# A trunk layer on one core: gate-and-up weights split 256 columns at once, and two of the second sub-layer's weight sums made in DRAM

## The chip, the cores and the metric

The kernel runs on one core of one Trainium2 chip. A core has a matrix engine (PE, with its weight loads listed as PEld), a vector engine (DVE), an activation engine (ACT), GpSimd (POOL) and a sync engine (SP) that issues transfers; each works through its own queue of instructions in a fixed order, and they wait for each other by semaphores. Data lie in DRAM, in SBUF (128 partitions) and in PSUM, the eight banks into which PE sums. The metric is the device time in microseconds (us) of one execution.

## The reference

One layer over 512 tokens of width 1024, all in float32, with three sub-layers, each between two RMS norms:

```python
x = x + 1/2 * PostNorm(SwiGLU_1(PreNorm(x)))   # gate and up: 1024 -> 2 x 2816, down: 2816 -> 1024
x = x +       PostNorm(Mixer(PreNorm(x)))      # pooling heads and sliding-window attention
x = x + 1/2 * PostNorm(SwiGLU_2(PreNorm(x)))

def swiglu(h, w_gu, w_down):
    gate, up = split(h @ w_gu, 2)
    return (silu(gate) * up) @ w_down
```

The change concerns the product `h @ w_gu` of the two SwiGLU sub-layers, named f1 and f2 in the kernel.

## The kernel before

**Numbers in two parts.** PE multiplies in a short format. So each float32 operand is split into a high part (a rounding copy, line 125 on ACT or 127 on DVE) and a low part (operand minus high part, line 128, on DVE or POOL), and each product of two 128x128 by 128xN blocks takes three matmuls (`mm3`, lines 304 to 306): high times high, high weight times low token part, low weight times high token part. The third of three is the first that needs the low part of the weights.

**Gate and up.** The columns of both halves are taken in 11 chunks of 256 (`CH`). Chunk 0 is multiplied block by block while the tokens are being normed (`block`, line 446). For the other ten, gate and up, each cut into two halves of features, make a two by two block matrix: a and b of gate, c and d of up, 512 features x 256 columns each, 0.5 MB. The tokens make the other one. Seven products take the place of eight (a form of Strassen's scheme by Winograd). Their weight operands are a (product 1), b (2), d (4), and four sums: s1 = c + d (5), s2 = s1 - a (6), s4 = b - s2 (3) and s3 = a - c (7). The sums of tokens are made once (`token_sums`); the sums of weights are made for each chunk by DVE (`makers`, lines 177 to 198), in chunk 1 by POOL.

The loop of lines 488 to 513 takes 128 columns at a time: of the seven products, each of 12 matmuls of 128x256 that sum into half a PSUM bank, in the order 1, then product 4 of the columns before (`finish`), then 2, 5, 6, 3, 7. Between them ACT and DVE copy partial results out of PSUM and add them up; DVE's sum after product 7 is line 512.

**Order of the weights' work.** `Weights` holds a list of operands in the order of use and makes an operand's parts when it is `AHEAD` = 4 operands ahead of the product being written; the two pools of parts hold `WB` = 12 tiles of 128x512. Loads are issued by SP, `run_ahead` loads ahead, each of 512 features x 256 columns, into `BIG` = 8 tiles of 0.5 MB. `behind` (line 435) lets a piece of work be issued only after certain steps. PE's queue stands in the order of the program; the other engines' queues, outside `in_order()`, stand in the order that a scheduler found while the program was built.

**The start.** Four blocks of 128 tokens are loaded, normed and turned (`first_steps`). The norm's root r_a of each block is made on POOL (line 279), and DVE then scales the block (line 323). POOL also makes low parts of the first weights there. r_a3, the root of the last block, stands ahead of half of the first columns' products.

Of the kernel before, what the change touches and what calls it, by code (L numbers as in the profile page):

```python
# [19 lines left out]
P = 128  # L20
S = 512
# [18 lines left out]
WB = 12  # L40
AB = 8
HB = 25
BIG = 8
AHEAD = 4
# [4 lines left out]
def shape_consts():  # L49
    """What depends on the shapes alone: the band of the sliding window, the count of tokens at the  # L50
    start of a trailing window, and the frequencies of the rotation."""
    c = np.zeros((P, CW), np.float32)
    i, j = np.arange(P)[:, None], np.arange(2 * P)[None, :]
    diff = i + P - j
    c[:, :256] = np.where((diff >= 0) & (diff < P), 0.0, NEG)
    for g, w in enumerate(WINDOWS):
        n = np.minimum(np.arange(16) + 1, w)
        c[:, 256 + 16 * g : 272 + 16 * g] = (np.float32(w) / n.astype(np.float32))[None, :]
    e = -np.arange(0, ROT, 2, dtype=np.float32) / np.float32(ROT)
    c[:, -8:] = np.power(np.float32(500000.0), e)[None, :]  # L60
    return c
# [3 lines left out]
def trunk_layer(  # L65
# [11 lines left out]
    pp = ctx.enter_context(tc.tile_pool(name="pp", bufs=8, space=PSUM))  # L77
# [6 lines left out]
    def bank(name):  # L84
        return pp.tile([P, 512], F32, tag="ps", name=name)
# [7 lines left out]
    # ---- weights, in the order of their use: each is split into two parts of 12 significant bits  # L93
    class Weights:
        def __init__(self):
# [3 lines left out]
            self.hi, self.lo = nc.scalar, nc.vector  # L99

        def add_load(self, key, src, shape):
            self.loads.append((key, src if isinstance(src, list) else [(slice(0, P), src)], shape))

        def add(self, name, make):
            """An operand: make() gives it in float32 once the loads added so far are there."""
            self.index[name] = len(self.todo)
            self.todo.append((name, len(self.loads), make))
# [8 lines left out]

        def make_to(self, n):
            while self.made < min(n, len(self.todo)):
                name, need, make = self.todo[self.made]
                self.load_to(need + self.run_ahead)  # L120
                src = make()
                hi = wp.tile(list(src.shape), F32R, tag="hi", name=f"{name}_hi")
                lo = wp.tile(list(src.shape), F32R, tag="lo", name=f"{name}_lo")
# [21 lines left out]
    def add_plain(key, src, shape, picks):  # L145
        W.add_load(key, src, shape)
        for name, at in picks:
            W.add(name, lambda at=at: W.raw[key][at])

    def add_gate_up(name, w_gu, c):  # L150
        def load(m, kh):
            c0 = m * FF + c * CH
            src = w_gu[0, kh * 512 : (kh + 1) * 512, c0 : c0 + CH]
            W.add_load(f"{name}_{c}{m}{kh}", src.rearrange("(k p) c -> p k c", p=P), [P, 4, CH])

        cut = [(slice(None), slice(None), slice(j * P, (j + 1) * P)) for j in range(2)]
        if c == 0:
            for m in range(2):
                load(m, 0)
                load(m, 1)  # L160
                for i in range(4):
# [3 lines left out]
                        lambda m=m, kh=kh, j=j: W.raw[f"{name}_0{m}{kh}"][cut[j]],  # L165
                    )
            return
        for m in range(2):
            for kh in range(2):
                load(m, kh)  # L170
        box = {}

        def parts(j):
            return [W.raw[f"{name}_{c}{m}{kh}"][cut[j]] for m in range(2) for kh in range(2)]

        def a11(j):
            r = parts(j)
            if j == 0:
                box["s1"] = big(f"{name}_{c}s1", (P, 4, CH))
            eng = nc.gpsimd if c == 1 else nc.vector  # L180
            eng.tensor_tensor(box["s1"][cut[j]], r[2], r[3], ALU.add)
            eng.tensor_tensor(r[2], r[0], r[2], ALU.subtract)  # L182
            return r[0]

        def s2(j):
            r = parts(j)
            nc.vector.tensor_tensor(r[0], box["s1"][cut[j]], r[0], ALU.subtract)
            return r[0]

        def s4(j):  # L190
            r = parts(j)
            nc.vector.tensor_tensor(r[1], r[1], r[0], ALU.subtract)  # L192
            return r[1]

        makers = (
            (1, a11), (2, lambda j: parts(j)[1]), (5, lambda j: box["s1"][cut[j]]), (6, s2), (3, s4),
            (7, lambda j: parts(j)[2]), (4, lambda j: parts(j)[3]),
        )
        for j in range(2):
            for p, make in makers:  # L200
                W.add(f"{name}_{c}{j}p{p}", lambda make=make, j=j: make(j))

    def add_ffn(name, w_gu, w_down):
        for c in range(NCH):
            add_gate_up(name, w_gu, c)
        for k in range(KF):
            add_plain(
                f"{name}_d{k}", w_down[0, k * P : (k + 1) * P, :], [P, D],
                [(f"{name}_d{k}{n}", (slice(None), slice(n * 512, (n + 1) * 512))) for n in range(2)],
            )  # L210

    def add_in(name, c0, w, kk, per):
        for q in range(KD // kk):
            src = w_in[0, q * kk * P : (q + 1) * kk * P, c0 : c0 + w]
            picks = [
                (f"{name}{(q * kk + i) // per}", (slice(None), i if per == 1 else slice(i, i + per)))
                for i in range(0, kk, per)
            ]
            add_plain(f"{name}_{q}", src.rearrange("(k p) c -> p k c", p=P), [P, kk, w], picks)

    # ---- what stays on chip
# [20 lines left out]
    rows = cp.tile([12, P], F32, name="rows")  # L242
# [5 lines left out]

    add_ffn("f1", ffn1_w_gu, ffn1_w_down)
    add_in("wq", PW, 512, 2, 1)  # L250
    add_in("wkv", 2 * PW, 256, 4, 2)
    add_in("wu", 0, 512, 2, 1)
    for n in range(2):
        ns = slice(n * 512, (n + 1) * 512)
        for q in (2, 3, 0, 1):
# [6 lines left out]
            picks = [(f"wo{n}{2 * q + i}", (slice(None), i)) for i in range(2)]  # L262
            add_plain(f"wo{n}_{q}", src, [P, 2, 512], picks)
# [12 lines left out]
    def power(ms, name):  # L276
        """ms ** -0.5"""
# [9 lines left out]
    def squares(parts, mult, name, split=False):  # L287
        """Sums of (mult * part) ** 2 of two halves of a block of tokens."""
        ss2 = sm.tile([P, 2], F32, tag="ss2", name=f"ss2_{name}")
        for n in range(2):  # L290
            if n == 1 and split:
                junk = wk.tile([P, 512], F32, tag="sg", bufs=2, name=f"j_{name}{n}")
# [8 lines left out]
    def mm3(ps, wl, xr, first, last, open_=False):  # L301
        """ps += w.T @ x from the parts of both."""
# [10 lines left out]
    # ---- norm of a block of tokens, and its transpose  # L313
# [37 lines left out]
    def post_norm(t, parts, g, scale, name, dst=None):  # L351
        """x += scale * norm(parts) * g for a block of tokens."""
# [30 lines left out]
    def evacuate(src, t, kh, xq):  # L383
        at = slice((t % 2) * P, (t % 2 + 1) * P)
        hi, lo = xq[0][kh, t // 2]
        nc.scalar.copy(hi[:, :, at], src)
        nc.vector.tensor_tensor(lo[:, :, at], src, hi[:, :, at].bitcast(F32), ALU.subtract)

    def keep(src, t, kh, xq):
        at = slice((t % 2) * P, (t % 2 + 1) * P)  # L390
        for q in range(2):
            nc.scalar.copy(xq[1][kh, t // 2][q][:, :, at], src[:, 2 * q : 2 * q + 2, :])
# [7 lines left out]
    def token_sums(xq, name):  # L400
        """The sums of quarters that the seven products take."""
# [5 lines left out]
        for q in range(2):  # L407
            b11, b12, b21, b22 = (full[i][q] for i in ((0, 0), (0, 1), (1, 0), (1, 1)))
            nc.vector.tensor_tensor(b11, b12, b11, ALU.subtract)
            nc.vector.tensor_tensor(b12, b22, b12, ALU.subtract)  # L410
            nc.vector.tensor_tensor(b22, b22, b11, ALU.subtract)
            nc.vector.tensor_tensor(b21, b21, b22, ALU.subtract)
# [9 lines left out]
    def product_late(ps, w, xt, first, last):  # L422
        """As product(), with the low part of the tokens last."""
# [6 lines left out]
    def product(ps, w, xt, first=True, last=True):  # L430
        for k in range(4):
            mm3(ps, (w[0][:, k], w[1][:, k]), (xt[0][:, k], xt[1][:, k]), first and k == 0, last and k == 3, True)
# [8 lines left out]
    def gate_up(name, xq, hs, between):  # L441
        """silu(x @ gate) * (x @ up), transposed. The first columns block by block as the tokens
        come; then, for 128 columns of both, the two by two blocks (gate, up; tokens) from seven
        products (Winograd's form of Strassen's)."""
# [20 lines left out]
        W.more(4)  # L465
        for j in range(2):
            sg = wk.tile([P, S], F32, tag="sg", bufs=2, name=f"{name}_s0{j}")
            nc.scalar.activation(sg, banks[0, j], AF.Silu)
            h = slot(f"{name}_h0{j}")
            nc.vector.tensor_tensor(h, banks[1, j], sg, ALU.mult)  # L470
            hs.append(h)

# [7 lines left out]

        def finish():
            ps, w, h, sg = last
            product(ps[:, a], w, xs_[4], False)
            on_dve.append(nc.vector.tensor_tensor(h[:, a], ps[:, a], sg[:, a], ALU.mult).ins)
            nc.vector.tensor_tensor(h[:, b], h[:, b], sg[:, b], ALU.mult)
            hs.append(h)

        for c in range(1, NCH):
            if c == NCH - 1:
                W.run_ahead = 2  # L490
            for j in range(2):
                nm = f"{name}_{c}{j}p"
                px, py, pz = (bank(f"{name}_{i}{c}{j}") for i in "xyz")
                sg = wk.tile([P, S], F32, tag="sg", bufs=2, name=f"{name}_s{c}{j}")
                h = slot(f"{name}_h{c}{j}")
                product(px[:, a], operand(f"{nm}1"), xs_[1], last=False)
                on_act.append(nc.scalar.copy(sg[:, a], px[:, a]).ins)
                if last:
                    finish()
                    if c == NCH - 1 and j == 0:  # L500
# [666 lines left out]
```

## Time and profile before

| | |
|---|---|
| time, median of 3 runs | 871.38 us (869.79 to 871.93) |
| profiled execution, span | 871.8 us |
| PE busy | 848.6 us, 97% |
| DVE busy | 628.8 us, 72% |
| ACT busy | 428.1 us, 49% |
| POOL busy | 104.6 us, 12% |
| moved by DMA | 87.35 MB, 100 GB/s on the mean |
| f1: start and first columns | 0 to 40.27 us |
| f1: gate and up, ten chunks | 40.27 to 241.95 us |
| f1: down | 242.1 to 363.7 us |
| mixer and output | to 516.4 us |
| f2: first columns | 516.4 to 543.5 us |
| f2: gate and up, ten chunks | 543.5 to 745.1 us |
| f2: down | 745.1 to 867 us |

The stages are told apart by what PE multiplies. The span is that of the one execution that the hardware profiler took; the median is that of three other runs. A row of a timeline has start, duration (both us), engine, line, operation, what it writes and reads by the program's names with buffer numbers left out, partitions x elements; then, in brackets, how long the engine had been idle and which instruction released it.

### The profile page before, as it was taken

How to read it: one execution, taken by the hardware profiler on the slowest of the kernel's cores; microseconds unless marked ns; L12 is line 12 of the kernel's file. 1: busy time of each engine (PE TensorE's matmuls, PEld its weight loads, DVE VectorE, ACT ScalarE, POOL GpSimd, SP SyncE). 2: the span in 40 equal slices, each digit the busy share in tenths (PEclk: the TensorE clock that was granted, in tenths of full speed). 3: DMA queues.
4: the chain of work that ended last, by engine and by line, in shares of the span. 5: the costliest groups of instructions: out<-in, count | busy, mean ns of one | idle time of the engine just before them, and what ended most of it. 6: DMA issues, size and time to landing. Idle time of an engine off the chain costs nothing. (4 is left out here: it accounts for less than half of the span.)

```text
span 871.8 us, 14391 instructions
## 1 busy us (share of the span) xinstructions
PE 848.6 (97%) x5633; PEld 775.9 (89%) x5633; DVE 628.8 (72%) x1177; ACT 428.1 (49%) x923; POOL 104.6 (12%) x124
## 2 busy tenths in 40 slices
PE   7999999999999999999989989999999999999996
PEld 5999999999988888888767779999999999888885
DVE  6988888888893223855998879988888888942214
ACT  6555555555583222637653356555555555832211
POOL 4300000000000000136464334000000000000000
PEclk9999999999999999999999999999999999999999
DMA  9333333333363333202023401333333333642002
GB/s 306 89 97 98 97 98 97 111 118 127 105 232 122 97 97 95 73 26 51 24 64 108 143 24 50 97 98 97 98 97 97 108 119 114 227 135 73 1 1 97
DMA packets 62448, 87.35 MB, mean 100 GB/s; under 512 B 3492, under 2 KB 50220, under 8 KB 62380
## 3 DMA queue, kind: packets, MB, share of 16 engines
q1 hardware_dynamic: 62380, 86.44, 31.0%
q8 instruction: 44, 0.72, 0.3%
q14 instruction: 24, 0.20, 0.1%
HBM read 84.33 MB, written 2.10 MB: 99 GB/s over the span
## 5 line engine op out<-in xcount | busy, mean ns | idle before, releaser
L304 PE MATMUL f_acc<-f_d_hi,f_hp_hi 128*128 128x512 f32 x352 | 137.4, 390 | 0.0
L306 PE MATMUL f_acc<-f_d_hi,f_hp_lo 128*128 128x512 f32 x352 | 137.1, 389 | 0.0
L305 PE MATMUL f_acc<-f_d_lo,f_hp_hi 128*128 128x512 f32 x352 | 137.1, 389 | 0.0
L128 DVE TENSOR_TENSOR f_d_lo<-f_d_raw,f_d_hi 128x512 fp32r<-128x512 f32 x88 | 58.9, 690 | 100.4 <-ACT f_d_hi L125 100.4
L125 ACT CAST f_d_hi<-f_d_raw 128x512 fp32r<-128x512 f32 x88 | 53.2, 621 | 108.6 <-PE f_acc L306 107.2
L304 PEld LDWEIGHTS f_acc<-f_d_hi,f_hp_hi 128*128 128x128 f32 x352 | 66.1, 188 | 13.7
L306 PEld LDWEIGHTS f_acc<-f_d_hi,f_hp_lo 128*128 128x128 f32 x352 | 66.1, 188 | 13.6
L305 PEld LDWEIGHTS f_acc<-f_d_lo,f_hp_hi 128*128 128x128 f32 x352 | 66.1, 188 | 13.6
L510 ACT ACTIVATE f_s<-f_s 128x512 f32<-128x512 f32 x40 | 25.3, 632 | 49.3 <-DVE f_s L509 49.2
L505 ACT COPY f_h<-f_y 128x256 f32<-128x256 f32 x40 | 14.9, 373 | 58.0 <-PE f_y L306 58.0
L279 POOL TENSOR_TENSOR r_f2po<-ms_f2po,half 128x1 f32<-128x1 f32 x4 | 2.2, 550 | 328.1 <-DVE ms_f2po L284 328.1
L279 POOL TENSOR_TENSOR r_f1po<-ms_f1po,half 128x1 f32<-128x1 f32 x4 | 2.2, 548 | 321.8 <-DVE ms_f1po L284 321.8
L512 DVE TENSOR_TENSOR f_h<-f_x,f_h 128x256 f32<-128x256 f32 x40 | 17.0, 424 | 31.3 <-PE f_x L306 31.3
L530 DVE TENSOR_TENSOR f_hp_lo<-f_h,f_hp_hi 128x512 fp32r<-128x512 f32 x44 | 27.9, 687 | 0.0
L192 DVE TENSOR_TENSOR f_raw<-f_raw,f_raw 128x512 f32<-128x512 f32 x40 | 27.5, 687 | 0.0
L304 PE MATMUL po<-wo_hi,yT_hi 128*128 128x512 f32 x64 | 26.4, 412 | 0.0
L305 PE MATMUL po<-wo_lo,yT_hi 128*128 128x512 f32 x64 | 25.8, 403 | 0.0
L306 PE MATMUL po<-wo_hi,yT_lo 128*128 128x512 f32 x64 | 25.7, 401 | 0.0
L507 ACT COPY f_s<-f_x 128x256 f32<-128x256 f32 x40 | 14.9, 373 | 21.9 <-PE f_x L306 21.9
L182 DVE TENSOR_TENSOR f_raw<-f_raw,f_raw 128x512 f32<-128x512 f32 x36 | 24.7, 687 | 0.0
L529 ACT CAST f_hp_hi<-f_h 128x512 fp32r<-128x512 f32 x44 | 24.6, 617 | 0.0
L298 ACT ACTIVATE j_f2po<-f_acc 128x512 bf16<-128x512 f32 x8 | 4.8, 597 | 27.3 <-PE f_acc L306 27.3
(1541 smaller groups left out, 3044.5 us busy)
## 6 DMA issues: line engine op xcount, KB each, us to landing
f_raw<-in_ffn_w_gu SPq DMA_DIRECT2D x88, 512.0 KB, 5.4
f_d_raw<-in_ffn_w_down SPq DMA_DIRECT2D x44, 512.0 KB, 4.5
x<-in_x SPq DMA_DIRECT2D x4, 512.0 KB, 8.2
wq_raw<-in_w_in SPq DMA_DIRECT2D x4, 512.0 KB, 3.6
wu_raw<-in_w_in SPq DMA_DIRECT2D x4, 512.0 KB, 3.7
wo_raw<-in_w_out SPq DMA_DIRECT2D x8, 256.0 KB, 4.0
wo_raw<-in_w_out SPq DMA_DIRECT2D x4, 512.0 KB, 3.6
out<-x SPq DMA_DIRECT2D x8, 256.0 KB, 2.1
```

Source lines behind the costliest of these rows:

```text
L125: nc.scalar.copy(hi, src)
L128: self.lo.tensor_tensor(lo, src, hi.bitcast(F32), ALU.subtract)
L182: eng.tensor_tensor(r[2], r[0], r[2], ALU.subtract)
L192: nc.vector.tensor_tensor(r[1], r[1], r[0], ALU.subtract)
L304: nc.tensor.matmul(ps, wh, xh, start=first, stop=False, skip_group_check=open_)
L305: nc.tensor.matmul(ps, wh, xlo, start=False, stop=False, skip_group_check=open_)
L306: nc.tensor.matmul(ps, wlo, xh, start=False, stop=last, skip_group_check=open_)
L505: on_act.append(nc.scalar.copy(h[:, b], py[:, a]).ins)
L510: on_act.append(nc.scalar.activation(sg, sg, AF.Silu).ins)
L512: on_dve.append(nc.vector.tensor_tensor(h[:, b], px[:, a], h[:, b], ALU.add).ins)
L529: nc.scalar.copy(hi[:, j], hs[2 * q + j])
L530: nc.vector.tensor_tensor(lo[:, j], hs[2 * q + j], hi[:, j].bitcast(F32), ALU.subtract)
```

## The change

Four things change together; the matmuls keep their number and shape.

First, a chunk's products take all 256 columns: the parts of an operand are tiles of 128x1024 (`WB` 6 of them, `AHEAD` 2), one product is 24 matmuls into two neighbouring banks (`bank_pair`, `use_banks`), and each of ACT's and DVE's steps on partial results is done for both halves, in one instruction or in two. The order of products is now 1, product 4 of the chunk before, 5, 2, 6, 3, 7.

Second, the signs of the tokens are turned (`evacuate`, `keep`, `token_sums`, and a scale of -1 in the activations), so that the weight sums become s2 = s1 + a, s4 = s2 + b: sums only. Chunk 1 of f1 has its sums on DVE like the others.

Third, for f2 the sums s1 and s3 of chunks 1 to 10 are made in DRAM: for each of four steps, POOL issues a copy of half of one operand's columns from DRAM to DRAM (512x1280, 2.62 MB, line 285) and two adding DMAs of 256x1280 (line 288). f2 then loads five blocks of 0.5 MB a chunk (a, b, s1, s3, d) in place of four.

Fourth, the weights of the mixer, the output projection and the down projections are also split in tiles of 128x1024.

```diff
-WB = 12
+WB = 6
-HB = 25
+HB = 24
-AHEAD = 4
+AHEAD = 2
...
+        made = sums_of.get(name)
+        if made:
+            cols = slice((c - 1) * CH, c * CH)
+            for i in made:
+                src[i] = made[i][:, cols].rearrange("(k p) c -> p k c", p=P)
...
+        def s1():
+            if not made:
+                raw[key["s1"]] = big(f"{key['s1']}", shape)
+                plus("s1", "c", "d")
+                plus("c", "a", "c")
+            return raw[key["s1"]]
+
+        def s2():
+            return plus("s1", "s1", "a") if made else plus("a", "s1", "a")
+
+        def s4():
+            return plus("s1", "s1", "b") if made else plus("b", "a", "b")
+
+        s3 = "s3" if made else "c"
+        for p, make in (
+            (1, lambda: raw[key["a"]]), (5, s1), (2, lambda: raw[key["b"]]), (6, s2), (3, s4),
+            (7, lambda: raw[key[s3]]), (4, lambda: raw[key["d"]]),
+        ):
+            W.add(f"{name}_{c}p{p}", make)
...
+    def sum_in_dram(step):
+        i, m, kh = (("s1", 1, 1), ("s3", 0, 0))[step // 2]
+        half = (FF - CH) // 2
+        at = slice(step % 2 * half, (step % 2 + 1) * half)
+        to = sums_of["f2"][i][:, at]
+        c0 = CH + step % 2 * half
+        nc.gpsimd.dma_start(to, ffn2_w_gu[0, :512, FF + c0 : FF + c0 + half])
+        part = ffn2_w_gu[0, kh * 512 : (kh + 1) * 512, m * FF + c0 : m * FF + c0 + half]
+        for rows in (slice(0, 256), slice(256, 512)):
+            nc.gpsimd.dma_start(to[rows], part[rows], accum_op=ALU.add)
...
+    def product(pair, half, w, xt, first=True, last=True):
+
+        for j in range(2):
+            at = slice(j * P, (j + 1) * P)
+            for k in range(4):
+                mm3(
+                    pair[:, j, half], (w[0][:, k, at], w[1][:, k, at]), (xt[0][:, k], xt[1][:, k]),
+                    first and k == 0, last and k == 3, True,
+                )
...
         for c in range(1, NCH):
             if c == NCH - 1:
                 W.run_ahead = 2
+            nm = f"{name}_{c}p"
+            if name == "f1" and 2 <= c < 6:
+                sum_in_dram(c - 2)
+            px = bank_pair(f"{name}_x{c}")
...
+            product(px, a, operand(f"{nm}1"), xs_[1], last=False)
+            on_act.append(nc.scalar.copy(sg[:, :, a], px[:, :, a]).ins)
+            if last:
+                finish()
...
+            product(px, a, operand(f"{nm}7"), xs_[7], False, False)
+            for j in range(2):
+                on_dve.append(nc.vector.tensor_tensor(h[j][:, b], px[:, j, a], h[j][:, b], ALU.add).ins)
+            last = (px, operand(f"{nm}4"), h, sg)
```

How the queues of POOL and DVE stand is set when the program is built, at three places as follows. POOL at the start of the program, before (r_a0 to r_a3 are the roots of the four blocks of tokens, f1_c the first columns' weights):

```order
L279 TENSOR_TENSOR r_a0_155<-ms_a0_153,half_96 128x1
L279 TENSOR_TENSOR r_a1_167<-ms_a1_165,half_96 128x1
L128 TENSOR_TENSOR f1_c000_lo_197<-f1_000_raw_102,f1_c000_hi_196 128x512
L128 TENSOR_TENSOR f1_c001_lo_205<-f1_001_raw_104,f1_c001_hi_204 128x512
L128 TENSOR_TENSOR f1_c010_lo_211<-f1_000_raw_102,f1_c010_hi_210 128x512
L128 TENSOR_TENSOR f1_c011_lo_215<-f1_001_raw_104,f1_c011_hi_214 128x512
L279 TENSOR_TENSOR r_a2_239<-ms_a2_237,half_96 128x1
L279 TENSOR_TENSOR r_a3_260<-ms_a3_258,half_96 128x1
L128 TENSOR_TENSOR f1_c111_lo_263<-f1_011_raw_109,f1_c111_hi_262 128x512
```

and after (sum_s1 and sum_s3 are the sums in DRAM; line 285 is a step's copy, 288 its adds):

```order
L285 DMA sum_s1_104<-in_ffn2_w_gu 512x1280
L285 DMA sum_s1_104<-in_ffn2_w_gu 512x1280
L285 DMA sum_s3_105<-in_ffn2_w_gu 512x1280 x2
L318 TENSOR_TENSOR r_a0_159<-ms_a0_157,half_96 128x1
L318 TENSOR_TENSOR r_a1_171<-ms_a1_169,half_96 128x1
L288 DMA sum_s1_104<-in_ffn2_w_gu 256x1280 x2
L156 TENSOR_TENSOR f1_c00_lo_201<-f1_000_raw_106,f1_c00_hi_200 128x4x128
L288 DMA sum_s1_104<-in_ffn2_w_gu 256x1280 x2
L156 TENSOR_TENSOR f1_c01_lo_209<-f1_001_raw_108,f1_c01_hi_208 128x4x128
...
L318 TENSOR_TENSOR r_a2_237<-ms_a2_235,half_96 128x1
L288 DMA sum_s3_105<-in_ffn2_w_gu 256x1280 x2
L318 TENSOR_TENSOR r_a3_258<-ms_a3_256,half_96 128x1
```

The four copies stand ahead of r_a0, and each step's adds, which wait until that step's copy is complete, stand between the roots and the low parts of the first weights; the third step's stand ahead of r_a3.

DVE where chunk 2 of f1 gives way to chunk 3, before (20 and 21, 30 and 31 are the two halves of 128 columns of chunks 2 and 3; 3s1 is a sum of weights, 30p1_lo the low part of product 1's operand, h and s partial results, x, y and z banks of PSUM):

```order
L128 TENSOR_TENSOR f1_21p4_lo_1014<-f1_211_raw_761,f1_21p4_hi_1013 128x512
L181 TENSOR_TENSOR f1_3s1_1038<-f1_310_raw_767,f1_311_raw_1030 128x4x128
L128 TENSOR_TENSOR f1_30p1_lo_1042<-f1_300_raw_763,f1_30p1_hi_1041 128x512
L182 TENSOR_TENSOR f1_310_raw_767<-f1_300_raw_763,f1_310_raw_767 128x4x128
L128 TENSOR_TENSOR f1_30p2_lo_1059<-f1_301_raw_765,f1_30p2_hi_1058 128x512
L509 TENSOR_TENSOR f1_s21_962<-f1_y21_960,f1_s21_962 128x256
L512 TENSOR_TENSOR f1_h21_963<-f1_x21_959,f1_h21_963 128x256
L187 TENSOR_TENSOR f1_300_raw_763<-f1_3s1_1038,f1_300_raw_763 128x4x128
L485 TENSOR_TENSOR f1_h21_963<-f1_h21_963,f1_s21_962 128x256
```

and after (h20 and h21 are chunk 2's two halves):

```order
L568 TENSOR_TENSOR f1_s2_769<-f1_y2_829,f1_s2_769 128x2x256
L572 TENSOR_TENSOR f1_h20_770<-f1_x2_768,f1_h20_770 128x256
L572 TENSOR_TENSOR f1_h21_771<-f1_x2_768,f1_h21_771 128x256
L211 TENSOR_TENSOR f1_3s1_989<-f1_3c_raw_726,f1_3d_raw_951 128x1024
L156 TENSOR_TENSOR f1_3p1_lo_960<-f1_3a_raw_722,f1_3p1_hi_959 128x1024
L535 TENSOR_TENSOR f1_h20_770<-f1_h20_770,f1_s2_769 128x256
L535 TENSOR_TENSOR f1_h21_771<-f1_h21_771,f1_s2_769 128x256
L211 TENSOR_TENSOR f1_3c_raw_726<-f1_3a_raw_722,f1_3c_raw_726 128x1024
L156 TENSOR_TENSOR f1_3p5_lo_993<-f1_3s1_989,f1_3p5_hi_992 128x1024
```

The low part of chunk 3's first operand stood four rows ahead of the sum out of x21 (line 512), which follows product 7. It now stands behind the two such sums (line 572) and s1.

DVE at the end of f2's first columns, before (f2t are sums of tokens, c10 and c11 the banks of the first columns' up half, h00 and h01 their results):

```order
L412 TENSOR_TENSOR f2f101_5767<-f2f101_5767,f2f111_5769 128x512
L470 TENSOR_TENSOR f2_h00_6223<-f2_c10_5992,f2_s00_6221 128x512
L128 TENSOR_TENSOR f2_10p3_lo_6236<-f2_101_raw_6189,f2_10p3_hi_6235 128x512
L419 TENSOR_TENSOR f2t6_lo_6160<-f2f111_5769,f2t6_hi_6159 128x512
L419 TENSOR_TENSOR f2t4_lo_6164<-f2f100_5766,f2t4_hi_6163 128x512
L470 TENSOR_TENSOR f2_h01_6227<-f2_c11_6017,f2_s01_6225 128x512
```

and after:

```order
L461 TENSOR_TENSOR f2t6_lo_5600<-f2f111_5209,f2t6_hi_5599 128x512
L461 TENSOR_TENSOR f2t4_lo_5604<-f2f100_5206,f2t4_hi_5603 128x512
L156 TENSOR_TENSOR f2_1p2_lo_5668<-f2_1b_raw_5629,f2_1p2_hi_5667 128x1024
L461 TENSOR_TENSOR f2t4_lo_5604<-f2f101_5207,f2t4_hi_5603 128x512
L519 SCALAR_TENSOR_TENSOR f2_h00_5653<-f2_c10_5426,f2_s00_5651 128x512
L519 SCALAR_TENSOR_TENSOR f2_h01_5657<-f2_c11_5455,f2_s01_5655 128x512
```

The rows that read the banks c10 and c11 stand behind all low parts of the token sums and a split of 128x1024; before, some of the token sums came after them.

More of the change, by code (lines that the diff above doesn't have):

```diff
@@ L185, in s2 @@
[L185 to L201, printed above, removed]
+        src = {"a": block(0, 0), "b": block(0, 1), "c": block(1, 0), "d": block(1, 1)}
@@ L545, in down_proj @@
                     h_pair(k // 2 + 1)
-                w = [W.get(f"{name}_d{k}{n}") for n in range(2)]
+                w = in_halves(W.get(f"{name}_d{k}"))
             for t in range(NT):
```

238 lines of the change are left out of this document (126 added, 112 removed).

## The prediction

> **What bounds the kernel now.** The page comes first: busy time by engine, then the slices.
>
> ```profile
> PE 848.6 (97%) x5633; PEld 775.9 (89%) x5633; DVE 628.8 (72%) x1177; ACT 428.1 (49%) x923; POOL 104.6 (12%) x124
> ...
> PE   7999999999999999999989989999999999999996
> ...
> DMA  9333333333363333202023401333333333642002
> GB/s 306 89 97 98 97 98 97 111 118 127 105 232 122 97 97 95 73 26 51 24 64 108 143 24 50 97 98 97 98 97 97 108 119 114 227 135 73 1 1 97
> ```
>
> PE is busy for 848.6 of 871.8 us. A change can win by issuing fewer matmuls, which this one doesn't, or out of the other 23 us; it can lose wherever it makes PE wait. The DMA is full in one slice only, the first. The windows say where the 23 us lie; columns are the busy time of each engine with its instructions, then the granted clock, the DMA share and GB/s.
>
> ```profile
> 0.00:22.00 22.00, 17.48 (x97) 12.89 (x98) 14.92 (x28) 13.13 (x32) 10.17 (x16) 0.92 0.96 306
> 22.00:40.27 18.27, 17.32 (x145) 16.91 (x144) 18.00 (x24) 11.20 (x24) 7.74 (x6) 1.00 0.35 103
> 100.00:150.00 50.00, 50.00 (x419) 50.00 (x418) 42.12 (x80) 27.17 (x55) 0.00 (x0) 1.00 0.27 85
> 441.00:516.40 75.40, 67.08 (x290) 53.37 (x289) 64.22 (x98) 30.18 (x67) 33.31 (x34) 0.93 0.28 85
> 516.40:543.50 27.10, 25.60 (x210) 24.84 (x208) 24.98 (x37) 15.72 (x37) 12.83 (x10) 1.00 0.19 60
> 543.50:745.10 201.60, 201.60 (x1683) 201.60 (x1681) 172.21 (x323) 111.26 (x226) 0.00 (x0) 1.00 0.34 108
> ```
>
> In gate and up PE has no gap: 1683 matmuls in 201.60 us, 0.12 us each, so a chunk of 256 columns (168 matmuls) is 20 us and one of its products (24 matmuls, both 128-column halves) 2.87 us. PE idles at the start (4.5 and 1 us) and in mixer and output (8.3 and 1.5). DVE has slack but it is 0.85 busy in gate and up, so what matters is the order in which its queue stands.
>
> **The new forms.** All products keep their 24 matmuls per 256 columns; PE does as much as before. Four splits of 128x512 become two of 128x1024, on DVE and ACT. The rows for DVE's sizes, and the place where one product hands over to the next, before:
>
> ```profile
> 109.27 0.28 PE L306 MATMUL f_x<-f1t_hi,f_40p_lo 128*128 128x256 f32 x1
> 109.39 0.28 PE L304 MATMUL f_x<-f1b_hi,f_41p_hi 128*128 128x256 f32 x1
> 109.62 0.28 PE L306 MATMUL f_x<-f1b_hi,f_41p_lo 128*128 128x256 f32 x1
> ```
>
> ```profile
> 106.26 0.69 DVE L128 TENSOR_TENSOR f_41p_lo<-f_raw,f_41p_hi 128x512 fp32r<-128x512 f32 x1
> ...
> 109.58 0.42 DVE L512 TENSOR_TENSOR f_h<-f_x,f_h 128x256 f32<-128x256 f32 x1 [0.93 <-PE f_x L306]
> 109.93 0.68 DVE L187 TENSOR_TENSOR f_raw<-f_4s,f_raw 128x512 f32<-128x512 f32 x1
> 110.52 0.42 DVE L485 TENSOR_TENSOR f_h<-f_h,f_s 128x256 f32<-128x256 f32 x1
> ```
>
> The last matmul of product 7 starts at 109.27, product 1 of the next columns at 109.39; its third matmul, the first with a low part, at 109.62, 0.23 later. DVE's sum out of PSUM (L512) starts 0.19 after the next product begins and gives way after 0.35 (109.58 to 109.93) though it lasts 0.42; a 128x512 gives way after 0.59 and lasts 0.68. By these slopes 128x1024 gives way after some 1.1 us and lasts 1.2 (estimates from these rows). Before, the low part of product 1 (the row at 106.26) began 3.4 us ahead of need.
>
> **Each chunk's first product: +26 in the first sub-layer, +17 in the second.** As built, the queue of DVE puts the low part of the next chunk's product 1 behind the two sums (now L572) that wait for the end of product 7, the product just before it; in the first sub-layer also behind the sum s1 (L211). Time is counted from the start of product 1: the sums start at 0.2 and 0.55, s1 at 0.9, the low part at 2.0, done at 3.2. Needed at 0.23. PE waits 3.0 us. Without s1 the low part starts at 0.9, done at 2.1: 1.85. What follows isn't late again, since DVE works on while product 1 and the held-back product 4 run, 5.7 us. In the first sub-layer chunk 2 has no s1 there (1.85) and chunks 3 to 10 do (8 x 3.0): 25.9. In the second s1 comes loaded: 9 x 1.85 = 16.7. Nothing hides these, for PE has no other product that it could take first. From below, the wait would be nothing only if DVE's order weren't fixed; it is. From above, 3.4 and 2.2, if a wait costs DVE another 0.35. The two sums that come ready from DRAM relieve a DVE that was hidden anyway: nothing.
>
> **The start: +26.** POOL before (its timeline), with the row of its longest wait:
>
> ```profile
> 11.07 6.28 POOL L128 TENSOR_TENSOR f_c_lo<-f_raw,f_c_hi 128x512 fp32r<-128x512 f32 x4 [0.84 <-ACT f_c_hi L125]
> 18.50 0.66 POOL L279 TENSOR_TENSOR r_a<-ms_a,half 128x1 f32<-128x1 f32 x1 [1.16 <-DVE ms_a L284]
> 20.96 1.27 POOL L279 TENSOR_TENSOR r_a<-ms_a,half 128x1 f32<-128x1 f32 x1 [1.80 <-DVE ms_a L284]
> 22.20 1.28 POOL L128 TENSOR_TENSOR f_c_lo<-f_raw,f_c_hi 128x512 fp32r<-128x512 f32 x1
> ```
>
> ```profile
> 22.27 3.46 DVE L323 SCALAR_TENSOR_TENSOR xn_a<-x,r_a,g 128x512 f32<-128x512 f32 x2 [0.45 <-POOL r_a L279]
> 30.31 0.68 DVE L387 TENSOR_TENSOR f1b_lo<-tr_f,f1b_hi 128x512 fp32r<-128x512 f32 x1
> ```
>
> ```profile
> 40.27 0.28 PE L304 MATMUL f_x<-f1b_hi,f_10p_hi 128*128 128x256 f32 x1
> ```
>
> The fourth block of tokens hangs on r_a3 on POOL (20.96 to 22.23), DVE scales it at 22.27, and gate and up start at 40.27, 18 us behind. The source puts the DMAs that make the sums into chunks 2 to 5 of the first sub-layer, where POOL stands idle. The built queue has them at its start: four copies from DRAM to DRAM of 2.62 MB each ahead of r_a0, and the adds between the small operations, each step's behind a wait for the copy that it adds to. The third step's adds stand ahead of r_a3, so r_a3, the last columns' low part and all that follows wait until three copies, 7.86 MB, have landed. Meanwhile the loads of x, gains and first weights need the same DMA: 22 us x 306 GB/s = 6.7 MB at a share of 0.96. Together 14.6 MB, at 306 GB/s 47.6 us; r_a3 then lets DVE scale at 48.3, 26 us after 22.27. That loads or copies go first matters little: if the copies do, the last of the loads that the first columns need lands as late. Below: the row of the only queue,
>
> ```profile
> q1 hardware_dynamic: 62380, 86.44, 31.0%
> ```
>
> moves 86.44 MB in 31.0% of 871.8 us, 320 GB/s while busy: 45.5 us, +24; less only if a copy is cheaper than a load. Above: if a copied byte costs twice, being read and written in DRAM, 22.4 MB, 73 us, +51. I take +26, since the rows show bytes moved once.
>
> The Trainium skill (DMA: Bandwidth & Descriptors, "Latency and other measured facts") has 207 to 214 GB/s for copies between HBM tensors in a good layout; by that figure, an estimate, 7.86 MB last 37 us beside 22 us of loads, the start would be +37 and the kernel 963 us. No row of this trace has a copy from DRAM to DRAM.
>
> **The adds beside the first sub-layer: +4.** The fourth copy and eight adds, 13.1 MB, run while gate and up load weights.
>
> ```profile
> f_raw<-in_ffn_w_gu SPq DMA_DIRECT2D x88, 512.0 KB, 5.4
> ```
>
> A load lands in 5.4 us and one is needed every 5 us, four per chunk. The DMA is 0.34 busy: 0.66 of 306 GB/s carry 13.1 MB in 65 us, so shared evenly it costs nothing. If the adds went ahead of all loads, 43 us less the three loads that are kept ahead (15 us) is +28. I take 4, nearest to the measured share.
>
> **The seams: +8.5.** First sub-layer: product 5 is now second (it was third), so its sum s1, the difference after it and its low part stand behind the token sums. Behind the last f1b_lo (done at 31.0) come 12 of 128x512 (0.6 each), 6 with a scalar (0.7, half of the pair below) and 4 of 128x1024 (1.1 each): 15.8, to 46.8; needed at 40.27 + 2.87 + 0.23 = 43.4: +3. Second: the first matmul of chunk 1 needs the bank of the first columns, which frees when f2_h01 has read it.
>
> ```profile
> 526.75 1.41 DVE L323 SCALAR_TENSOR_TENSOR xn_c<-x,r_c,g 128x512 f32<-128x512 f32 x2 [0.44 <-POOL r_c L279]
> 528.08 0.42 DVE L127 CAST f_c_hi<-f_raw 128x512 fp32r<-128x512 f32 x1
> 528.42 1.28 DVE L387 TENSOR_TENSOR f2b_lo<-tr_f,f2b_hi 128x512 fp32r<-128x512 f32 x2
> ...
> 545.78 0.68 DVE L470 TENSOR_TENSOR f_h<-f_c,f_s 128x512 f32<-128x512 f32 x1
> ```
>
> ```profile
> 543.50 0.28 PE L304 MATMUL f_x<-f2b_hi,f_10p_hi 128*128 128x256 f32 x1
> ```
>
> Before, nothing waited for that row at 545.78. From 528.1 DVE now does 3 casts (0.33), 4 of 128x1024, 12 of 128x512 and 10 with a scalar ahead of the bank's release: 19.6, to 547.7, against 543.5: +4. At the ends of gate and up the last columns are finished by pairs before a bank goes to the next stage: two more sums of 0.35 and their wait, 1.5 in both together. Half of all these may be hidden, or as much again be added by semaphores: 4 to 12.
>
> **Mixer and output: 0.** Their weights are split by 128x1024 in queues of DVE and POOL that other steps stand in; a step caught behind one waits up to 0.6 us longer, and fewer instructions give back as much. The 8.3 us of idle there are the bound of a gain; I keep -4 to +4. The loads of the second sub-layer's sums wait on SP for adds that end before 250 us, and are due near 500: nothing. The token signs, the wider scratch and the smaller pools add no work to PE.
>
> **The sum.** 26 + 26 + 17 + 4 + 8.5 = 81 on a span of 871.8, whose execution is 0.4 above the median of 871.38: 952. What a measurement of this kernel can tell from no change is about 0.3%, 2.6 us.
>
> **The rivals.**
> Copies are dear (each byte counts twice and they go ahead of the loads): start +51, adds +28, 952 + 25 + 24 = 1001; 977 if only the start suffers. For it: the DMA at 0.96 with loads alone. Against it: 0.34 from then on. Chance 0.25.
> The start is cheap (the copies land beside the loads before r_a3 is due at 21 us): 952 - 26 = 926. Against: 7.86 MB would have to land in 21 us beside 6.7 MB, 690 GB/s. Chance 0.12.
> The chunks hide their first split (a low part that DVE reaches in time): 952 - 43 = 909. Against: DVE's order is fixed. Chance 0.07.
> Faster: DVE has less to do in output and in the second sub-layer's first columns, where the windows leave PE idle for 8.3 + 1.5 us; wider splits close that, and the result is 862. It decides if product 1's third matmul comes at 0.3 us or less after its first and copy 3 lands before 21 us, so that nothing stands against it. Chance 0.03.
> That the sums aren't made beside idle POOL, but at the start, is part of the forecast.
>
> **How the numbers follow.** The forecast itself has 0.52. The range 915 to 1005 takes in its bounds (start 24 to 51, adds to 28, seams 4 to 12, mixer 4 each way), the dear copies and the cheap start; left out are hidden chunks and a gain, and part of what runs into both dear terms. Faster 0.03, same 0.01 (the tail of that), slower 0.96.
>
> **What would show it.** Right: POOL with r_a3 near 47 us behind a DMA; gate and up starting at some 66 us; in each chunk one PE gap at the third matmul of product 1, released by DVE's L156, of 3.0 us in the first sub-layer and 1.85 in the second; a period of 23.0 and 21.9 us where there were 20.0. Wrong: gate and up start before 50, or a chunk stays at 20.0, or its gaps are released by DMA.

## The result, and the profile after

The changed kernel takes 1031.26 us (median of 4 runs, 1030.25 to 1031.43) against 871.62 us before: 1.183 times as long, with a 95% interval of 1.181 to 1.184. The direction was as forecast; the size was twice what was forecast, and lies outside the range. The profiled execution has a span of 1029.4 us, 157.6 more than before.

From the page of the profile after: busy time, three of the slices, and the two DMA queues, of which q0 is new.

```profile
PE 878.6 (85%) x5633; PEld 798.0 (78%) x5633; DVE 582.9 (57%) x843; ACT 395.3 (38%) x671; POOL 103.3 (10%) x122
...
PE   2114788888888899999999899799999999999997
...
PEclk6556798999899899999999999899999999999999
DMA  9879652222223263332120250414333444453002
...
q1 hardware_dynamic: 67660, 91.68, 28.8%
q0 software_dynamic: 4288, 20.97, 8.2%
```

PE issues the same 5633 matmuls, but is busy for 30 us more, 18 of them in gate and up of f1 and 7 in gate and up of f2. (The granted clock, PEclk, is at 8 tenths in some slices there; the 5 to 7 tenths of the first five slices are read while PE mostly stands idle.) DVE has 46 us less to do, and nothing comes of it. The DMA is busy at 6 tenths or more in all of the first five slices (129 us), where before it was at 9 tenths in the first and at 3 in the next four. The windows put times to the stages (columns as in the prediction).

```profile
0.00:46.00 46.00, 5.25 (x14) 1.78 (x14) 1.19 (x5) 2.93 (x6) 3.35 (x12) 0.60 0.91 323
46.00:126.10 80.10, 34.43 (x224) 32.64 (x225) 27.83 (x46) 20.70 (x48) 15.66 (x17) 0.64 0.78 167
126.10:373.30 247.20, 219.83 (x1683) 215.99 (x1681) 165.45 (x204) 99.67 (x130) 0.90 (x1) 0.93 0.32 94
373.30:496.60 123.30, 121.80 (x547) 101.02 (x547) 55.86 (x77) 44.12 (x73) 2.76 (x5) 1.00 0.34 105
496.60:641.80 145.20, 138.65 (x755) 114.14 (x754) 112.97 (x239) 77.36 (x204) 68.07 (x76) 1.00 0.22 64
641.80:679.47 37.67, 29.83 (x210) 27.94 (x208) 31.21 (x45) 17.28 (x36) 10.33 (x8) 0.91 0.33 99
679.47:902.00 222.53, 208.66 (x1680) 205.56 (x1681) 138.36 (x168) 97.92 (x126) 0.00 (x0) 0.98 0.38 116
```

| stage | before, us | after, us | more |
|---|---|---|---|
| start and first columns of f1 | 40.3 | 126.1 | +85.8 |
| gate and up of f1 | 201.7 | 247.2 | +45.5 |
| down of f1 | 121.7 | 123.3 | +1.6 |
| mixer, output, first columns of f2 | 179.8 | 182.9 | +3.1 |
| gate and up of f2 | 201.6 | 222.5 | +20.9 |
| down of f2, end | 126.7 | 127.4 | +0.7 |

**The start.** POOL's timeline (of the long waits, only these rows):

```profile
1.34 0.86 POOL L285 DMA_DIRECT2D sum_s<-in_ffn_w_gu  x1 [0.33 <-issue]
...
17.79 0.67 POOL L285 DMA_DIRECT2D sum_s<-in_ffn_w_gu  x1 [15.17 <-issue]
32.22 0.62 POOL L285 DMA_DIRECT2D sum_s<-in_ffn_w_gu  x1 [13.75 <-issue]
45.60 0.63 POOL L285 DMA_DIRECT2D sum_s<-in_ffn_w_gu  x1 [12.77 <-issue]
46.24 0.60 POOL L318 TENSOR_TENSOR r_a<-ms_a,half 128x1 f32<-128x1 f32 x1
...
95.48 0.93 POOL L288 DMA_DIRECT2D sum_s<-in_ffn_w_gu  x1 [4.91 <-issue]
106.78 0.90 POOL L288 DMA_DIRECT2D sum_s<-in_ffn_w_gu  x1 [10.37 <-issue]
107.37 0.92 POOL L318 TENSOR_TENSOR r_a<-ms_a,half 128x1 f32<-128x1 f32 x1
```

Ahead of each later DMA POOL stands idle, 13 to 15 us ahead of the copies and 5 to 10 us ahead of the adds. The releaser reads "issue": the profile shows nothing that POOL waited for, and no semaphore. The copies were to be handed over at once and only the adds to wait; instead each DMA stands at the head of POOL's queue until about the time that the one before it is through. r_a0 comes behind the fourth copy (46.24, before 5.58), r_a3 behind the sixth add (107.37, before 20.96). Gate and up start 18.7 us after it; before it was 19.3.

**The chunks.** PE where chunk 4 of f1 follows chunk 3, and the waits of PE (us in total, times, longest):

```profile
198.20 0.28 PE L344 MATMUL f_x<-f1b_lo,f_4p_hi 128*128 128x256 f32 x1
201.16 0.39 PE L345 MATMUL f_x<-f1b_hi,f_4p_lo 128*128 128x256 f32 x1 [2.67 <-DVE f_4p_lo L156]
201.38 0.28 PE L343 MATMUL f_x<-f1b_hi,f_4p_hi 128*128 128x256 f32 x1
```

```profile
PE tr_f L417 <- DVE xn_a L362: 53.2, 3, 41.2
PE f_c L468 <- POOL f_c_lo L156: 35.1, 4, 16.5
...
PE f_x L345 <- DVE f_4p_lo L156: 4.2, 2, 2.7
...
PE f_y L343 <- ACT f_2p_hi L153: 3.1, 1, 3.1
```

The third matmul of product 1 comes 2.96 us after the second where 0.12 is its due: 2.84 lost. The row of f_4p_lo holds both sub-layers, 2.7 + 1.5. Chunks 3 to 10 of f1 lose 2.84 each and chunk 2 1.70, 24.4 in all; nine chunks of f2 lose 1.70 each, 15.3.

The wait for f_2p_hi, in product 5 of chunk 2, is 4.2 us with 0.9 behind it. It looks like a late load, since s1 needs the last block of the chunk, but DVE's rows say otherwise:

```profile
152.12 0.76 DVE L533 TENSOR_TENSOR f_h<-f_x,f_s 128x256 f32<-128x256 f32 x2 [5.19 <-PE f_x L345]
152.79 1.22 DVE L211 TENSOR_TENSOR f_2s<-f_2c_raw,f_2d_raw 128x1024 f32<-128x1024 f32 x1
```

In DVE's queue s1 of chunk 2 (L211) stands behind the two products with the results of product 4 (L533). DVE is idle for 5.2 us until PE is through product 4, and s1 then starts with no wait for a load. So this too is the order of DVE's queue.

What remains of the two stages' 45.5 and 20.9 us, beside 0.7 at the seam, is matmuls at a slower pace, 16.2 and 5.6 us more than before. So they look in f2, after a wait that ended at 721.13; below them the windows of the matmuls just behind that wait and of the slow ones:

```profile
722.37 0.41 PE L345 MATMUL f_x<-f2b_hi,f_3p_lo 128*128 128x256 f32 x1
722.58 0.41 PE L343 MATMUL f_x<-f2b_hi,f_3p_hi 128*128 128x256 f32 x1
```

```profile
721.13:722.30 1.17, 1.17 (x9) 1.17 (x10) 1.17 (x3) 0.00 (x0) 0.00 (x0) 0.97 0.00 0
722.30:725.30 3.00, 3.00 (x16) 3.00 (x15) 1.72 (x2) 0.00 (x0) 0.00 (x0) 0.50 0.00 0
```

They come every 0.21 us instead of every 0.12, for 3 us, and the granted clock is at 0.50; it fell 1.1 us after the wait had ended.

### The profile page after: what moved, and what is told of

Same layout as the page of the kernel before. It is cut to its first block, busy times and chain, and to the rows that moved or that the text cites. A ratio compares the mean times of both kernels' runs of the same rounds, so it can differ in the third digit from the quotient of the medians.

```text
span 1029.4 us, 13798 instructions
## 1 busy us (share of the span) xinstructions
PE 878.6 (85%) x5633; PEld 798.0 (78%) x5633; DVE 582.9 (57%) x843; ACT 395.3 (38%) x671; POOL 103.3 (10%) x122
## 3 DMA queue, kind: packets, MB, share of 16 engines
q0 software_dynamic: 4288, 20.97, 8.2%
## 5 line engine op out<-in xcount | busy, mean ns | idle before, releaser
L156 DVE TENSOR_TENSOR f_d_lo<-f_d_raw,f_d_hi 128x1024 fp32r<-128x1024 f32 x44 | 53.7, 1223 | 90.8 <-ACT f_d_hi L153 90.8
L153 ACT CAST f_d_hi<-f_d_raw 128x1024 fp32r<-128x1024 f32 x44 | 45.9, 1053 | 100.3 <-PE f_acc L345 100.3
L362 DVE SCALAR_TENSOR_TENSOR xn_a<-x,r_a,g 128x512 f32<-128x512 f32 x8 | 6.7, 872 | 90.2 <-POOL r_a L318 90.2
L417 PE MATMUL tr_f<-ident,xn_a 128*128 128x128 f32 x32 | 7.2, 390 | 53.3 <-DVE xn_a L362 53.2
L417 PEld LDWEIGHTS tr_f<-ident,xn_a 128*128 128x128 f32 x32 | 5.5, 201 | 54.7 <-DVE xn_a L362 43.0
L533 DVE TENSOR_TENSOR f_h<-f_x,f_s 128x256 f32<-128x256 f32 x36 | 13.6, 420 | 59.5 <-PE f_x L345 59.5
L468 PE MATMUL f_c<-f1b_hi,f_c_lo 128*128 128x256 f32 x64 | 18.5, 315 | 31.9 <-POOL f_c_lo L156 31.9
L468 PEld LDWEIGHTS f_c<-f1b_hi,f_c_lo 128*128 128x128 f32 x64 | 14.1, 221 | 32.5 <-POOL f_c_lo L156 32.5
L553 ACT COPY f_s<-f_x 128x512 f32<-128x512 f32 x20 | 11.7, 587 | 71.8 <-PE f_x L345 69.8
L569 ACT ACTIVATE f_s<-f_s 128x1024 f32<-128x1024 f32 x20 | 21.2, 1059 | 39.8 <-DVE f_s L568 39.8
```

Source lines behind the costliest of these rows:

```text
L153: nc.scalar.copy(hi, src)
L156: self.lo.tensor_tensor(lo, src, hi.bitcast(F32), ALU.subtract)
L417: nc.tensor.transpose(ps[:, k * P : (k + 1) * P], xn[kh][:, k * P : (k + 1) * P], ident)
L468: nc.tensor.matmul(ps, w[1][:, k], xt[0][:, k], start=False, stop=False)
L533: on_dve.append(nc.vector.tensor_tensor(h[j][:, a], px[:, j, a], sg[:, j, a], ALU.mult).ins)
L569: on_act.append(nc.scalar.activation(sg, sg, AF.Silu, scale=-1.0).ins)
```

## The experiments

Ratios are to the kernel before in runs on the same chip (872 to 873 us). The first group asks what holds up the start, the second what costs the chunks, the third what the DMAs cost elsewhere.

**ring5: more room for descriptors.** A parameter of the kernel sets the room in SBUF for the descriptors of GpSimd's DMAs; it is made five times as large, and two scratch tiles pay for it.

```diff
-HB = 24
+HB = 22
...
-dynamic_dma_scratch_size=1024
+dynamic_dma_scratch_size=5120
```

> The changed kernel with five times the room for the descriptors of GpSimd's DMAs (and two fewer scratch tiles, which pay for it); order of the queues unchanged. Theory A (POOL can have one such DMA in flight, so r_a3 stands behind the end of four copies and five adds): the four copies are issued within 10 us, r_a3 waits only for copy 3 to land, near 50 us instead of 107, gate and up start near 68 instead of 126, about 970 us. Rival B (the DMA engines' bytes are the limit, whoever waits): r_a3 comes after 85 us all the same, 1010 to 1031 us.

1019.58 us, ratio 1.166 (1.162 to 1.171). POOL's timeline and the windows:

```profile
2.54 1.87 POOL L285 DMA_DIRECT2D sum_s<-in_ffn_w_gu  x3
6.21 0.57 POOL L318 TENSOR_TENSOR r_a<-ms_a,half 128x1 f32<-128x1 f32 x1 [1.79 <-DVE ms_a L323]
...
61.49 0.68 POOL L318 TENSOR_TENSOR r_a<-ms_a,half 128x1 f32<-128x1 f32 x1 [15.30 <-DVE ms_a L323]
```

```profile
20.00:40.00 20.00, 9.95 (x50) 8.88 (x51) 3.33 (x6) 4.85 (x11) 6.79 (x6) 0.63 1.00 352
...
80.00:100.00 20.00, 1.22 (x11) 1.02 (x9) 0.00 (x0) 0.00 (x0) 0.00 (x0) 0.65 1.06 225
```

The four copies are now issued within 4.4 us, r_a0 comes at 6.21, and r_a3 at 61.49, 46 us sooner; there it waits for DVE, which waits for x: the load of the last block of tokens takes 43.3 us to land (16.1 in the change, 10.7 in late). So it was the room for descriptors that held POOL; late_hb22 and late_ring5 below change the room alone and agree. The mechanism of theory A stands and its time doesn't: the DMA is full (1.00 to 1.06 in the windows) until past 100 us, and although gate and up start at 78.2, loads come late there and PE waits 58.8 us in that stage where it waited 29 to 31. Of the 48 us won at the start 12 remain. Rival B is right about the time: the sums' bytes need the DMA, whoever waits.

**late: the same DMAs behind the start.** The twelve DMAs are queued on POOL behind r_a3 and the low part after it, the last two of a list of POOL's steps of the start.

```diff
+        pool_ops.append(nc.gpsimd.tensor_tensor(r, ms, half, ALU.pow).ins)
...
-                sum_in_dram(c - 2)
+                with behind(pool_ops[-2:]):
+                    sum_in_dram(c - 2)
```

> The changed kernel with the same DMAs queued on POOL behind r_a3 and the last low part of the first columns. Theory A: the start is that of before, gate and up from 40 us, 86 us less: 945 us, plus what the adds cost the loads beside them; 950 if they share evenly, up to 973 if the adds starve the loads. Rival B (bytes are the limit): the 80 us of DMA work come back as waits for loads in the first chunks, 980 us or more. The waits at each chunk's first product (2.84 and 1.70 us) stay in both.

944.72 us, ratio 1.083 (1.080 to 1.086): 86.5 us less than the change, as theory A has it. Gate and up start at 39.75. The DMAs go out one at a time between 24 and 149 us, beside the loads of the first chunks. One wait of 4.2 us is found there, in product 5 of chunk 3, and it is DVE's order again: the last load that s1 needs was issued at 67.35 and landed 7.5 us later, and s1 starts at 88.21, behind the products with product 4. So no load came late. (nosums below, without these DMAs, lacks this wait; why the scheduler placed s1 differently was not tried.)

**bef_start and bef_late: the DMAs alone.** The kernel before, with the twelve DMAs added in the one place or the other and their sums not read.

> The kernel before with the twelve DMAs alone added, in the place in POOL's queue that they have in the changed kernel; nothing reads their sums. Theory A (the start is lost to the place of these DMAs alone, and nothing else of the change has a part in it): gate and up start near 126 us, 86 later than before: some 957 us, up to 965 if the last adds hold up loads. Rival (the changed kernel's own start, wider splits and other signs, is part of it): 900 to 940 us.

> The kernel before with the same twelve DMAs behind r_a3 on POOL; nothing reads their sums. Theory A (one such DMA at a time leaves the loads enough of the DMA): 871 to 876 us. Rival B (some 100 us of DMA work hold up the loads of the first chunks): 885 us or more. Two sums of chunk 1 stand on POOL behind these DMAs in this kernel, so a wait for them in chunk 1 may show, up to 12 us, and is no wait for loads.

bef_start: 970.34 us, ratio 1.111 (1.108 to 1.115). Gate and up start at 124.78, 84.5 later than before: the start is lost to the DMAs' place alone. The time is 13 us over the expected 957 and 5 over the upper end given. These 13 us lie in gate and up of f1: four waits, 7.8 us, at the sums of chunk 1 (POOL, behind the adds) and of chunk 2 (DVE), and slower matmuls, 5 us.

bef_late: 916.05 us, ratio 1.049 (1.046 to 1.052): not as theory A has it, and in the range of rival B, though mostly not for B's reason. Its rows of POOL and of PE's waits:

```profile
57.16 0.63 POOL L263 DMA_DIRECT2D sum_s<-in_ffn_w_gu  x1 [9.48 <-issue]
57.80 2.50 POOL L184 TENSOR_TENSOR f_1s<-f_raw,f_raw 128x512 f32<-128x512 f32 x2
```

```profile
PE f_y L322 <- ACT f_10p_hi L125: 18.2, 1, 18.2
```

The sums of chunk 1, on POOL in this kernel, ran at 23.58 before and now at 57.80, behind four copies. A wait for them was expected to cost up to 12 us, and it cost 27 in three waits. Two waits in chunk 2, 3.4 us, are those of bef_start, where DVE takes the sums late. Loads cost 4.8 us, in chunks 4 and 5, where DVE waits for them; some 7 us are slower matmuls. It is the fault of the changed kernel's start once more, in another place: a small step behind a DMA that holds its queue.

**late_lag2: the next split one step earlier.** `LAG` sets behind which step on ACT and DVE the next operands' splits may be queued.

```diff
-LAG = 1
+LAG = 2
```

> As late, and the splits of the next operands may be queued one step earlier, so that DVE makes the next chunk's first low part ahead of the sums behind product 7. Theory C (these waits cost 24 + 15 us, and the drops of the granted clock that follow them another 16 + 6): both go, clock 1.00 in gate and up, late minus some 55 us: 890 to 900 us. Rival D (the clock drops for another reason, as the wide splits or the DMA's load): only the waits go, late minus 38, and the clock in gate and up stays near 0.92.

884.83 us, ratio 1.014 (1.011 to 1.016): 60 us less than late, 5 better than the range of theory C. As built, DVE has the low part of each next product 1 ahead of the sums behind product 7. Windows of late, then of late_lag2, gate and up of f1 and of f2:

```profile
39.75:282.22 242.47, 215.09 (x1684) 211.21 (x1682) 166.11 (x210) 101.90 (x133) 8.48 (x10) 0.96 0.61 166
587.62:814.64 227.02, 213.16 (x1681) 210.06 (x1681) 138.37 (x168) 97.93 (x126) 0.00 (x0) 0.96 0.37 114
```

```profile
39.72:248.78 209.06, 204.13 (x1683) 203.35 (x1682) 164.65 (x210) 100.52 (x132) 8.48 (x10) 0.99 0.70 193
554.75:756.44 201.69, 201.69 (x1680) 201.69 (x1681) 139.39 (x168) 98.12 (x126) 0.00 (x0) 1.00 0.42 131
```

f2 is back at 201.7, the time before, with a clock of 1.00, and f1 at 209, with the wait of 4.2 us in chunk 3 still there. The waits at product 1 are gone, and with them nearly all slow matmuls, with the same wide splits and the same DMAs: theory C.

**late_fill: work in place of a wait.** To part the two, each chunk of f2 gets matmuls whose results aren't used, where PE would wait.

```diff
+                for i in range(FILL[name]):   # f1: 0, f2: 14
+                    nc.tensor.matmul(
+                        pz[:, i % 2, b], w7[0][:, i % 4, :P], xs_[7][0][:, i % 4], start=True, stop=True,
+                        skip_group_check=True,
+                    )
```

> As late, with 14 matmuls of 128x256 into an unused half of a bank behind product 7 of each chunk of the second sub-layer, 1.67 us, where PE would wait 1.70 us; their results are not used. Theory E (the granted clock drops because PE stands idle): the waits are filled, the clock is 1.00 in gate and up of the second sub-layer, and the stage takes 217 us where it took 227: 935 us, faster with more work on PE. Rival D (the clock drops for another reason): 227 us or more, 945 to 950.

939.03 us, ratio 1.076 (1.072 to 1.080), 5.7 less than late with 126 matmuls more. Gate and up of f2:

```profile
594.42:814.07 219.65, 219.07 (x1807) 217.25 (x1808) 138.45 (x168) 98.15 (x126) 0.00 (x0) 1.00 0.38 118
```

The stage takes 219.65 us where late took 227.02, with the clock at 1.00. The order of DVE's queue is the same, so theory E holds: the clock drops because PE stands idle, be it for 1.7 us in 22. (f1, unchanged, took 6.6 us longer than in late, all in slower matmuls, and the total is 4 us over the expected 935. Not every wait is followed by a slow stretch: of the nine in f2 two are in the change and five in late. What decides it was not tried.)

**nosums and nosums_lag2: without the sums in DRAM.** f2 makes its sums on DVE, as f1 does; the second one has `LAG = 2` as well.

> The changed kernel without the sums in DRAM: the second sub-layer makes its sums on DVE as the first does. Theory A: the start is that of before, no adds beside the first sub-layer; the wait per chunk is 2.84 us in both sub-layers, 9 more than after in the second, and the clock's drops with it: 1031 - 86 - 4 + 10 + 5 to 10, about 960 us. Rival (the sums in DRAM relieve nothing and cost nothing but their place): within 3 us of late.

> Wide splits alone: no sums in DRAM, and the next operands' splits may be queued one step earlier. Theory: without the chunks' waits DVE carries the sums beside PE as it did before, so that the sums in DRAM relieve nothing: 880 to 884 us, 1 to 5 less than late_lag2 (884.83), since no adds hold up loads. Rival (the two sums fewer are what lets DVE keep up): the second sub-layer's gate and up take over 205 us where late_lag2 has 201.7, 887 us or more.

nosums: 957.79 us, ratio 1.099 (1.096 to 1.103), as theory A has it, and 13 more than late: with DVE's order at fault, s1 in front of the low part costs f2 what it costs f1 (239.3 us against 227.0). nosums_lag2: 881.14 us, ratio 1.010 (1.006 to 1.013): with the order right the sums in DRAM are worth nothing. They spare f2's gate and up 1.5 us (203.2 without them, 201.7 in late_lag2), and f1's gate and up take 5.9 us more with them. This is the fastest kernel with the wide splits, and is still 1% slower than the kernel before.

**late_hb22 and late_ring5: room for descriptors, beside the loads.** late with the two scratch tiles fewer, and with the larger room on top.

> As late, with two scratch tiles fewer and nothing else: the ground for late_ring5. 940 to 948 us; POOL issues a DMA of the sums every 10 to 13 us from 24 to 155 us. If the tiles matter, ring5's loss beside the loads is theirs in part.

> As late_hb22, with five times the room for the descriptors of GpSimd's DMAs. Theory F (with little room one such DMA at a time is in flight, and it is this that leaves the loads their share; the DMA's bytes are the limit once all go at once): the copies are issued together near 24 us, the DMA is full for some 80 to 100 us, loads come late, and PE waits some 28 us more in the first sub-layer's gate and up, as in ring5: 965 to 980 us. Rival G (the DMA shares evenly however many are in flight): within 5 us of late_hb22.

946.56 us, ratio 1.085 (1.081 to 1.088), and 961.19 us, ratio 1.101 (1.098 to 1.104). The tiles cost nothing that can be told from late. With more room the four copies go out at once and 14.6 us are lost, half of what theory F gave, at one place; the time is 4 us under its range. Windows of late_hb22, then of late_ring5, and PE's longest wait in the latter:

```profile
80.00:100.00 20.00, 14.59 (x83) 13.84 (x82) 11.43 (x14) 4.80 (x8) 1.80 (x2) 0.75 0.78 158
```

```profile
80.00:100.00 20.00, 7.02 (x55) 6.47 (x53) 3.31 (x7) 1.27 (x2) 0.00 (x0) 0.78 1.06 225
```

```profile
PE f_y L346 <- ACT f_3p_hi L153: 17.5, 1, 17.5
```

The DMA is full. The load of f_3d, for chunk 3, takes 35.2 us to land where it took 5.8 in late_hb22; DVE waits 14.3 us for it, and PE 17.5. (The 3.1 us that PE waits at that place in late_hb22 are DVE's order.) With more of these DMAs in flight the loads land later: theory F, at half its price.

## Why the prediction was wrong

**The step that failed** is in the start: "r_a3, the last columns' low part and all that follows wait until three copies, 7.86 MB, have landed". It counted the semaphore waits that stand in POOL's queue and took the issue of a DMA for free. With the room as built, about one of these DMAs is in flight; the next stands at the head of POOL's queue, and all behind it, until the one before has landed. (An add has half of a copy's rows, and adds go one at a time too; how much of the room each takes, the runs don't show.) r_a3 so waited for four copies and five adds, not for three copies: +85.8 us instead of +26. ring5 (r_a3 46 us earlier), late (86.5 us less) and bef_start (+84.5 with nothing else changed) show it.

Even with room the term would not have been +26. The prediction had the DMA carry 14.6 MB and stop there; but the adds start as soon as the first copies are in, and compete with the loads of x. ring5's start is +38, and 28 us more of waits follow in f1. The two bounds of the term, 24 and 51, held the bytes and left the queue out.

**The chunks** were right, in place and cause, and nearly in size: 3.0 and 1.85 us forecast, 2.84 and 1.70 measured; 26 + 17 forecast, 24.4 + 15.3 measured.

**The clock** wasn't in the sum. A wait was priced at its own length; some are followed by a stretch at a clock of 0.50, with matmuls every 0.21 in place of 0.12 us, 21.8 us in the two stages. Gate and up of the kernel before has no wait and so no such row, but the prediction's own window of 441.00 to 516.40, with 8.3 us of idle PE and a clock of 0.93, pointed to it.

**The adds beside the loads**: 4 forecast, and 4.2 found in the change and in late, but by luck: those 4.2 us are DVE's order (s1 behind the products with product 4), and no load came late. The forecast's premise, even sharing, holds only with few of these DMAs in flight: ring5 and late_ring5 show loads that land 35 to 60 us after their issue when many are. It is the want of room, the same that ruined the start, that keeps this term small: no wait for a load in late, 4.8 us in bef_late. The change itself hardly tests the term, since its last add has landed by 136.3 us, 10 us after gate and up start.

**The seams and the mixer**: 8.5 and 0 forecast. The seam into f1 gave 0.7 us instead of 3 (0.35 in late, whose start is that of before, so the term was too large; why was not tried); the ends of gate and up and the way from mixer to f2 gave 1.6, 3.1 and 0.7, with the mixer 7.5 us shorter and the first columns of f2 10.6 longer, where splits on POOL and DVE now come late. Why each of those two moved was not tried apart.

Together: 85.8 + 24.4 + 15.3 + 21.8 + 4.2 + 6.1 = 157.6, the measured difference; the 21.8 is what the waits leave of the two stages.

**The rivals.** "Copies are dear" had the side of it, but by bytes that count twice. For the copies this is not so. The fourth copy ran with no load beside it (window; the last columns are DMA share and GB/s):

```profile
45.60:55.72 10.12, 4.62 (x17) 3.29 (x17) 7.90 (x15) 5.84 (x14) 2.22 (x3) 0.50 0.79 259
```

That is 2.62 MB at 259 GB/s and a share of 0.79, some 330 GB/s at full share, no less than the 320 of the loads. The Trainium skill (DMA: Bandwidth & Descriptors, "Latency and other measured facts") has 207 to 214 GB/s at full rate for copies between HBM tensors that SP or ACT issue; this copy, issued from GpSimd, was faster, and the measurement decides. The adds are dear: 1.31 MB every 10 us.

## What to carry to other kernels

Before a DMA is put into an engine's queue, ask what that engine does behind it: here a transfer that nobody needed for 500 us stood ahead of a step of less than 1 us on which the whole start hung. An order that a scheduler chose should be read in the built queue, and pinned behind the urgent steps where it isn't right. And a wait of PE can cost more than its length, since matmuls after it can run slower: 44.6 us of waits in gate and up came with 21.8 us of slower matmuls here. A wait that looks like a late load should be followed back on the engine between: here DVE had the block and took it late.

## What the runs showed of the hardware

In these runs a DMA of GpSimd's for whose descriptors there was no room blocked POOL, while the profile named no releaser. The wait reads "issue", 5 to 15 us long. With the parameter at 1024 about one copy of 512 rows was in flight, with 5120 all four.

The changed kernel while it waits for one adding DMA alone (window; the last columns are DMA share and GB/s):

```profile
75.50:85.00 9.50, 0.00 (x0) 0.00 (x0) 0.00 (x0) 0.00 (x0) 0.88 (x1) 0.50 0.76 138
```

1.31 MB take 9.5 us, 138 GB/s, and the DMA is 0.76 busy: some 180 GB/s at full share (an estimate), against 320 for the loads of the kernel before and some 330 for a copy. So an added byte cost nearly twice a copied one. All sums together took 8.2% of 1029.4 us, 84 us of all 16 engines, for 20.97 MB.

The granted clock reacted to waits of 1.7 us in periods of 22 (0.96 over the stage in late, 1.00 in late_fill), though not to each of them. The Trainium skill (TensorE: Matmul & The Clock Gate, "Why this matters for your kernels") asks for no idle gaps over about 3 us between bursts; by the traces here shorter ones are enough, and the measurement decides.
